# Moving three small tiles so that the 52 general slots start at another address residue

## The chip, the core and the metric

The kernel runs on one core of a Trainium2 chip. The metric is the device time of one execution in microseconds, as the median of several runs. TensorE does the matmuls, VectorE and ScalarE the elementwise work, GpSimd and SyncE mostly issue DMAs. All operands of TensorE come from SBUF, the on-chip memory, in which every tile has a start address that is the same in each of 128 partitions.

## What is computed

One inference step of a one-layer decoder: 2048 prompt positions with 16 learned tokens ahead of them, and 8 sample positions. Cut to what matters:

```python
h = rmsnorm(x); p = h @ w_in            # q | k | v | conv GLU a | conv GLU b
attn = sliding-window attention(q, k, v)  # 8 heads, window 128, sinks, relative bias
c = silu(layernorm(depthwise_conv(a * sigmoid(b), width=31)))
x = x + concat(attn, c) @ w_out         # 1024 -> 1024
x = x + relu(rmsnorm(x) @ w_up)**2 @ w_down   # 1024 -> 4096 -> 1024
y = rmsnorm_final(x)
```

All arrays are float32. The outputs are y for prompt and samples, and the new key, value and convolution states.

## The kernel before, in words

Activations lie with the channels on the partitions and the tokens along the row. The tokens are cut into five tiles of 384, 448, 448, 448 and 320 prompt positions; the first has 16 more columns in its input projection (400), the last 8 sample columns (328). The program goes through the tiles, and the feed-forward of one tile covers attention and convolution of the next, whose steps are dealt out between matmuls by generators.

Weights come as 86 slabs of 128 x 1024: 14 for the input projection, 8 for the output projection and 64 for the feed-forward (up and down). dma_slab loads a slab into raw, and split_slab splits it on ScalarE and VectorE into whi and wlo, two float32r tiles whose sum is the slab. Activations are split the same way into a high and a low tile. pe_step multiplies one slab with one tile: 24 matmuls, of which 16 have whi as weights against the high and the low activation of 8 chunks, and 8 have wlo against the high one. The moving operands are general slots in the input projection, up and down. In the output projection four of the eight chunks are parts of the tiles cah and cal (attention) and four are general slots (convolution).

SBUF is dealt out by pools in the order in which they are opened (lines 80 to 84): cp for constants, tp for the general slots, tm for temporaries, sl for weight slabs, at for attention and the rest. Inside a pool the tiles follow in the order of their first use. A general slot comes from slot() in line 140, is 128 x TS float32, and has the name t; TS is 448, and there are 52 of them. A temporary comes from tmp() in line 144, has the name m and 448 columns too; ss and rs are of the same size. The small parameters sm hold the norm gains, the taps and biases of the convolution and the sinks, 169 columns, and are read as scalars of one column by VectorE and ScalarE all through the program. The constants epst and sq0 have one column each, idn, ones and onesr 128 columns, bias 8 x 256. In tp, relt is the first user of a slot.

The order of the instructions on each engine comes from the framework's scheduler. x is loaded into slots by DMA from SyncE or GpSimd (load_x, line 339), and the result is stored from slots in final_gen (line 908), for the last tile from SyncE and ScalarE by turns.

Of the kernel before, what the change touches and what calls it, by code (L numbers as in the profile page):

```python
# [7 lines left out]
F32 = mybir.dt.float32  # L8
# [31 lines left out]
NSMALL = 169  # L40
# [36 lines left out]
def trunk(tc, x_in, w_all, smalls, rel, ck, cv, sconv, y_out, kv_out, ck_out, cv_out, up_out, us_out):  # L77
    nc = tc.nc
    with ExitStack() as ctx:
        cp = ctx.enter_context(tc.tile_pool(name="cp", bufs=1))  # L80
        tp = ctx.enter_context(tc.tile_pool(name="tp", bufs=NSLOT))
        tm = ctx.enter_context(tc.tile_pool(name="tm", bufs=NTMP))
# [46 lines left out]
        def act(out, a, f, bias=0.0, scale=1.0, accum_out=None):  # L129
            if accum_out is None:  # L130
                return nc.scalar.activation(out, a, f, bias=bias, scale=scale)  # L131
            return nc.scalar.activation(out, a, f, bias=bias, scale=scale, accum_out=accum_out)  # L132
# [22 lines left out]
        def mm(out, lhsT, rhs, start, stop):  # L155
            return nc.tensor.matmul(out, lhsT, rhs, start=start, stop=stop)  # L156

        sm = cp.tile([128, NSMALL], F32, name="sm")
        nc.scalar.dma_start(sm, smalls)
        relt = tp.tile([128, TM], F32, tag="t", name="relt")  # L160
        nc.gpsimd.dma_start(relt[:33, :8 + EW], rel)
# [1 line left out]
        make_identity(nc, idn)  # L163
        ones = cp.tile([128, 128], F32, name="ones")
        nc.vector.memset(ones, 1.0)
        epst = tm.tile([128, 1], F32, tag="epst", name="epst", bufs=1)
        nc.vector.memset(epst, EPS)
        sq0 = tm.tile([128, 1], F32, tag="sq0", name="sq0", bufs=1)
        act(sq0, epst, AF.Sqrt)
        bias = cp.tile([128, NH, 256], F32, name="bias")  # L170
        scr = dr.tile([NSMP, NH, EW], F32, name="scr")
# [1017 lines left out]
def build(shapes):  # L1189
    import concourse.bacc as bacc  # L1190

    nc = bacc.Bacc("TRN2", target_bir_lowering=False, num_devices=1, dynamic_dma_scratch_size=8192)
    args = [nc.dram_tensor(n, s, F32, kind="ExternalInput").ap() for n, s in shapes.items()]
    args += [nc.dram_tensor(n, s, F32, kind="ExternalOutput").ap() for n, s in _OUTS]
    with tile.TileContext(nc, schedule_with_timeline_sim=True) as tc:
        trunk(tc, *args)
    return nc
# [28 lines left out]
```

## Time and profile before

| | us |
|---|---|
| median of 3 runs | 2118.57 |
| lowest and highest of them | 2117.73, 2121.74 |
| profiled execution, whole | 2122.0 |
| profiled execution, span | 2120.2 |
| TensorE busy in the span | 2086.2 |
| VectorE busy | 1525.5 |
| ScalarE busy | 1180.9 |

The span runs from the first to the last instruction. Busy time of an engine is the time in which one of its instructions was running; matmuls overlap, and their ends are modelled, so the distance between their starts tells the pace and the duration doesn't. The chain is the work that ended last, followed back from the end.

### The profile page before, as it was taken

To read this page: it belongs to the slowest core of one execution; us is meant where nothing else is said; L and a number is where in the kernel's file an instruction comes from. 1 tells how busy PE (TensorE), PEld (TensorE's weight loads), DVE (VectorE), ACT (ScalarE), POOL (GpSimd) and SP (SyncE) were. 2 spreads that over 40 slices of the span, in tenths; PEclk is the share of its full clock that TensorE was granted. 3 is DMA by queue.
4 is the path that set the end of the run, shared out by engine and by line. 5 is a ranking of instruction groups with operands and counts; after the bars stand their busy time and mean duration, and the time that the engine had idled before them with its cause. 6 is when DMAs were issued, how large, how long until landed. Compare 5 with 4: busy or idle time off the path is not lost.

```text
span 2120.2 us, 29986 instructions
## 1 busy us (share of the span) xinstructions
PE 2086.2 (98%) x11338; PEld 1967.8 (93%) x11338; DVE 1525.5 (72%) x2595; ACT 1180.9 (56%) x2156; POOL 50.7 (2%) x98
## 2 busy tenths in 40 slices
PE   7899999999999999999999999999999999999998
PEld 7787999999999999999999999999999999999997
DVE  5897698987857987648669886566797754574444
ACT  6576465567456455565455647554646475454443
POOL 2000000000000000000000000000010100000000
PEclk9999999999999999999999999999999999999999
DMA  5112333334533222234432222244433322444443
GB/s 203 42 40 80 110 123 116 120 110 154 179 112 102 100 99 100 100 131 148 144 110 100 100 100 100 100 170 145 147 115 112 121 100 103 151 161 153 148 143 104
DMA packets 77328, 254.19 MB, mean 120 GB/s; under 512 B 9501, under 2 KB 19869, under 8 KB 77184
## 3 DMA queue, kind: packets, MB, share of 16 engines
q1 hardware_dynamic: 72000, 238.08, 32.6%
q0 software_dynamic: 4464, 13.45, 1.9%
q8 instruction: 89, 1.46, 0.3%
q10 hardware_dynamic: 720, 0.76, 0.1%
q14 instruction: 55, 0.45, 0.1%
HBM read 241.97 MB, written 10.28 MB: 119 GB/s over the span
## 4 chain that ended last, share of the span: by engine, by line
PE 97%; DVE 2%; DMA 1%; ACT 0%; issue 0%; SPq 0%; DVEq 0%; ACTq 0%
PE mm L156 91%; PE st L156 2%; PE s L156 1%; PE pt L581 1%; PE cps L156 1%; DVE t L116 1%; DMA raw<-w_all 0%; DVE t L112 0%; DMA sm<-smalls 0%; DVE m L116 0%; DVE wlo L112 0%; ACT bias L135 0%; DVE ss L112 0%; PE mx L156 0%; PE st L530 0%
## 5 line engine op out<-in xcount | busy, mean ns | idle before, releaser
L156 PE MATMUL mm<-t,whi 128*128 128x448 f32 (+3 forms) x6560 | 1347.6, 352 | 14.0 <-ACT t L131 8.9
L156 PEld LDWEIGHTS mm<-t,whi 128*128 128x128 f32 x6560 | 1173.9, 189 | 76.3 <-ACT t L131 9.9
L135 ACT CAST whi<-raw 128x1024 fp32r<-128x1024 f32 x424 | 443.7, 1049 | 561.9 <-PE mm L156 444.3
L156 PE MATMUL mm<-t,wlo 128*128 128x448 f32 (+3 forms) x3280 | 709.0, 349 | 0.0
L112 DVE TENSOR_TENSOR wlo<-raw,whi 128x1024 fp32r<-128x1024 f32 x424 | 517.1, 1220 | 244.3 <-PE mm L156 138.2
L156 PEld LDWEIGHTS mm<-t,wlo 128*128 128x128 f32 x3280 | 588.8, 188 | 29.8 <-issue 0.6
L116 DVE SCALAR_TENSOR_TENSOR t<-u,sm,t 128x448 f32<-128x448 f32 (+1 forms) x480 | 301.1, 646 | 3.5
L112 DVE TENSOR_TENSOR t<-mm,t 128x448 f32<-128x448 f32 (+2 forms) x200 | 116.8, 584 | 182.8 <-PE mm L156 179.8
L112 DVE TENSOR_TENSOR t<-m,t 128x448 fp32r<-128x448 f32 (+3 forms) x236 | 134.5, 583 | 26.3 <-ACT t L135 25.7
L135 ACT CAST t<-m 128x448 fp32r<-128x448 f32 (+3 forms) x236 | 125.4, 536 | 18.7 <-DVE m L116 14.6
L131 ACT ACTIVATE m<-mm 128x448 f32<-128x448 f32 (+2 forms) x176 | 90.1, 512 | 53.1 <-PE mm L156 51.2
L131 ACT ACTIVATE m<-t 128x448 f32<-128x448 f32 (+3 forms) x140 | 72.3, 543 | 60.8 <-DVE t L112 40.9
L131 ACT ACTIVATE m<-m 128x448 f32<-128x448 f32 (+3 forms) x164 | 90.1, 550 | 9.0 <-DVE m L112 5.1
L132 ACT ACTIVATE p<-p,nm 112x240 f32<-112x240 f32 (+3 forms) x152 | 72.3, 477 | 26.8 <-DVE nm L121 26.6
L562 DVE CUSTOM_DVE_ANT_0 p<-s,bias,sm 112x240 f32<-112x240 f32 (+3 forms) x152 | 61.3, 450 | 4.6 <-PE s L156 2.7
L131 ACT ACTIVATE p<-p,rd 112x240 f32<-112x240 f32 (+3 forms) x152 | 61.9, 476 | 3.7 <-DVE rd L127 3.0
L112 DVE TENSOR_TENSOR ss<-ss,m 128x448 f32<-128x448 f32 (+3 forms) x100 | 58.5, 585 | 6.9 <-ACT m L131 3.4
L127 DVE RECIPROCAL rs<-m 128x448 f32<-128x448 f32 (+2 forms) x15 | 41.6, 2776 | 24.0 <-ACT m L131 24.0
L116 DVE SCALAR_TENSOR_TENSOR t<-t,sm 128x384 f32<-128x384 f32 (+1 forms) x98 | 56.9, 613 | 2.4 <-ACT t L131 2.0
L156 PE MATMUL mm<-cah,whi 128*128 128x448 f32 (+2 forms) x160 | 55.6, 349 | 1.2 <-DVE t L116 1.2
L920 POOL DMA_DIRECT2D y_out<-t x32 | 17.3, 542 | 1632.6 <-DVE t L116 1631.2
L156 PE MATMUL mm<-cal,whi 128*128 128x448 f32 (+2 forms) x160 | 55.4, 348 | 0.0
(179 smaller groups left out, 1145.4 us busy)
## 6 DMA issues: line engine op xcount, KB each, us to landing
raw<-w_all SPq DMA_DIRECT2D x424, 512.0 KB, 3.2
t<-x_in SPq DMA_DIRECT2D x40, 224.0 KB, 4.3
y_out<-t POOLq DMA_DIRECT2D x24, 224.0 KB, 3.3
t<-x_in SPq DMA_DIRECT2D x16, 164.0 KB, 3.5
t<-x_in POOLq DMA_DIRECT2D x8, 224.0 KB, 6.5
t<-x_in SPq DMA_DIRECT2D x8, 200.0 KB, 5.2
t<-x_in SPq DMA_DIRECT2D x8, 192.0 KB, 4.4
y_out<-t POOLq DMA_DIRECT2D x8, 192.0 KB, 3.9
```

The costliest lines, as they stand in the source:

```text
L112: return nc.vector.tensor_tensor(out, a, b, op=op)
L116: return nc.vector.scalar_tensor_tensor(out, a, s, b, op0=op0, op1=op1)
L127: return nc.vector.reciprocal(out, a)
L131: return nc.scalar.activation(out, a, f, bias=bias, scale=scale)
L132: return nc.scalar.activation(out, a, f, bias=bias, scale=scale, accum_out=accum_out)
L135: return nc.scalar.copy(out, a)
L156: return nc.tensor.matmul(out, lhsT, rhs, start=start, stop=stop)
L562: nc.vector.tensor_tensor_reduce(out=p[:bq, c, :nk], in0=sp[c // 2][:bq, c % 2, :nk], in1=bias[:bq, h, b0:b0 + nk], scale=1.0, scalar=sm[: ...
L581: nc.tensor.transpose(t[:r, c * bq:(c + 1) * bq], p[:bq, c, a:a + r], idn[:bq, :bq])
L920: q.dma_start(y_out[:, YO[i] + c * n:YO[i] + (c + 1) * n], y[:, :n])
```

## The change

Three tiles change their pool. sm goes from cp to tm, where it is the first to be allocated, with a tag and one buffer of its own. epst and sq0 go from tm to cp, behind ones. Nothing that writes or reads them is changed. The general slots, in the pool between the two, get another start address.

```diff
-        sm = cp.tile([128, NSMALL], F32, name="sm")
+        sm = tm.tile([128, NSMALL], F32, tag="sm", name="sm", bufs=1)
         nc.scalar.dma_start(sm, smalls)
         relt = tp.tile([128, TM], F32, tag="t", name="relt")
...
         nc.vector.memset(ones, 1.0)
-        epst = tm.tile([128, 1], F32, tag="epst", name="epst", bufs=1)
+        epst = cp.tile([128, 1], F32, name="epst")
         nc.vector.memset(epst, EPS)
-        sq0 = tm.tile([128, 1], F32, tag="sq0", name="sq0", bufs=1)
+        sq0 = cp.tile([128, 1], F32, name="sq0")
         act(sq0, epst, AF.Sqrt)
```

## Rows read from the trace of the kernel before

**Rows 1.** The page: busy time by engine, and granted clock in 40 slices.
```profile
PE 2086.2 (98%) x11338; PEld 1967.8 (93%) x11338; DVE 1525.5 (72%) x2595; ACT 1180.9 (56%) x2156; POOL 50.7 (2%) x98
...
PEclk9999999999999999999999999999999999999999
```

**Rows 2.** The page: the chain's shares by engine, then by line.
```profile
PE 97%; DVE 2%; DMA 1%; ACT 0%; issue 0%; SPq 0%; DVEq 0%; ACTq 0%
PE mm L156 91%; PE st L156 2%; PE s L156 1%; PE pt L581 1%; PE cps L156 1%; DVE t L116 1%; DMA raw<-w_all 0%; DVE t L112 0%; DMA sm<-smalls 0%; DVE m L116 0%; DVE wlo L112 0%; ACT bias L135 0%; DVE ss L112 0%; PE mx L156 0%; PE st L530 0%
```

**Rows 3.** Chain in order of time: start us, length us, what, number of instructions.
```profile
275.20 12.75 PE mm L156 x72
...
322.57 13.87 PE mm L156 x80
...
410.85 17.82 PE mm L156 x102
...
662.81 14.56 PE mm L156 x72
...
1001.01 29.93 PE mm L156 x148
...
1892.86 214.81 PE mm L156 x1432
```

**Rows 4.** Groups by shape, matmuls of 448 columns: out<-moving,weights, busy us, mean ns.
```profile
L156 PE MATMUL mm<-t,whi 128*128 128x448 f32 x3936 | 867.5, 367 | 1.0 <-DVE m L112 1.0
...
L156 PE MATMUL mm<-t,wlo 128*128 128x448 f32 x1968 | 455.8, 365 | 0.0
...
L156 PE MATMUL mm<-cal,whi 128*128 128x448 f32 x96 | 34.9, 364 | 0.0
L156 PE MATMUL mm<-cah,whi 128*128 128x448 f32 x96 | 34.9, 364 | 0.0
...
L156 PE MATMUL mm<-cah,wlo 128*128 128x448 f32 x96 | 23.4, 366 | 0.0
```

**Rows 5.** Timeline of TensorE, an output step of 448 columns: start us, us.
```profile
1004.30 0.37 PE L156 MATMUL mm<-cah,whi 128*128 128x448 f32 x1
...
1005.91 1.78 PE L156 MATMUL mm<-t,whi 128*128 128x448 f32 x8
1007.52 0.98 PE L156 MATMUL mm<-cah,wlo 128*128 128x448 f32 x4
1008.34 0.98 PE L156 MATMUL mm<-t,wlo 128*128 128x448 f32 x4
1009.15 0.37 PE L156 MATMUL mm<-cah,whi 128*128 128x448 f32 x1
```

**Rows 6.** Timeline of TensorE, starts of two output steps of 328 columns.
```profile
1808.88 0.32 PE L156 MATMUL mm<-cah,whi 128*128 128x328 f32 x1
...
1812.46 0.32 PE L156 MATMUL mm<-cah,whi 128*128 128x328 f32 x1
```

**Rows 7.** Groups by shape, VectorE and ScalarE on slots (t) and temporaries.
```profile
L112 DVE TENSOR_TENSOR t<-m,t 128x448 fp32r<-128x448 f32 x144 | 87.4, 620 | 18.2 <-ACT t L135 17.8
L135 ACT CAST t<-m 128x448 fp32r<-128x448 f32 x144 | 80.7, 567 | 15.3 <-DVE m L116 12.8
...
L112 DVE TENSOR_TENSOR m<-ss,m 128x448 fp32r<-128x448 f32 x11 | 6.8, 622 | 1.6 <-ACT m L135 1.6
...
L135 ACT CAST m<-ss 128x448 fp32r<-128x448 f32 x11 | 6.2, 563 | 2.2 <-DVE ss L112 2.2
```

**Rows 8.** Chain in order of time, head of the program.
```profile
0.81 4.34 DMA sm<-smalls
...
6.25 9.77 DMA raw<-w_all
```

**Rows 9.** The page, DMA issues: size of each, median us to landing.
```profile
y_out<-t SPq DMA_DIRECT2D x4, 164.0 KB, 1.9
y_out<-t ACTq DMA_DIRECT2D x4, 164.0 KB, 1.9
...
sm<-smalls ACTq DMA_DIRECT2D x1, 84.5 KB, 4.3
...
relt<-rel POOLq DMA_DIRECT2D x1, 50.5 KB, 4.6
```

## The prediction, made before the changed kernel ran

> **What bounds the kernel now.** I read the page first: TensorE is busy 98% of a span of 2120.2 us, and its granted clock stands at nine tenths or more in all 40 slices [rows 1]. The chain of work that ended last agrees: 97% of it is TensorE, 91% the one matmul line of the helper mm [rows 2]. So the time is the number of matmuls times their pace, and a change of addresses matters if it changes that pace, or the short head and tail where TensorE waits. The chain in order of time gives the pace, as microseconds of an unbroken piece divided by its matmuls [rows 3]. With 448 columns it is 14.56 us / 72 = 202.2 ns, with 328 columns 214.81 / 1432 = 150.0 ns. With 384 columns it differs from piece to piece: 13.87 / 80 = 173.4 ns, 17.82 / 102 = 174.7 ns, 12.75 / 72 = 177.1 ns. The columns alone, one for each cycle at the level of 2.4 GHz, would be an estimated 186.7, 136.7 and 160.0 ns. The pace thus carries 15.5 ns a matmul on top of 448 columns, and 13.3 to 17.1 ns on top of the others. An address can only act on this excess.
>
> **The change part by part.** First where things lie, from the shapes in the code. Tiles are laid one after the other in the order in which their pools are opened, in steps of 32 bytes a partition. Ahead of the general slots there were sm (676, so 704 bytes), idn, ones and onesr (512 each) and bias (8192), 10432 bytes in all. Now there are idn, ones, onesr, bias and the two constants of 32 bytes, 9792 in all. The slots move down by 640 bytes, which is 128 modulo 256. As they land on 192, they were on 64. A slot is 448 x 4 = 1792 bytes, seven times 256, so all 52 lie alike before and after. Behind them, the pool tm loses 64 bytes and gains 704 in front of the tiles m, so m, ss, rs, the weights raw, whi and wlo, and all of the pool at stay where they were. Counting on from the slots: m, ss, rs and the weights lie at 128, and in the pool at, behind the two small rq tiles, cah and cal lie at 192. That is the useful fact. The output projection reads moving operands from cah and cal, at 192, and from slots, at 64, in the same step and against the same weights. The kernel before therefore already runs matmuls on the address class to which the slots go.
>
> The change adds no instruction, no wait and no byte. sm is still written once by the same DMA, in the same program position; epst and sq0 have the same writers and readers. Edits other than addresses cost nothing by count.
>
> 448 columns, three of the five tiles: 3 x 86 slabs x 24 = 6192 matmuls. Mean durations by shape are 367 and 365 ns for slots and 364, 364 and 366 ns for cah and cal [rows 4]. Durations overlap, so the pace is the test. One output step takes 8 matmuls from cah and cal from 1004.30 to 1005.91, 1.61 us; 8 from slots to 1007.52, 1.61 us; 4 from cah to 1008.34, 0.82 us; 4 from slots to 1009.15, 0.81 us [rows 5]. The whole step is 4.85 us, and a step with slots alone is 14.56 / 3 = 4.85 us [rows 3]. A longer piece of the chain, from 1001.01 on, has 148 matmuls, among them 48 on cah or cal in its four output steps, and runs at 29.93 / 148 = 202.2 ns [rows 3]. Half or a third of the operands at 192 changes nothing to a tenth of a nanosecond. I take 0 us for 6192 matmuls. The bounds are in the rivals, since no stretch has all operands at 192.
>
> 328 columns, the last tile: 86 x 24 = 2064 matmuls. An output step with half of its operands at 192 goes from 1808.88 to 1812.46, 3.58 us [rows 6]; a step on slots alone is 24 x 150.0 = 3.60 us [rows 3]. If the 0.02 us belong to the class 192 and double when all operands are there, the 78 steps that now use slots alone gain 0.04 and the 8 others 0.02 us: about 3.3 us at most by rows rounded to 0.01 us. If they belong to the switching between classes inside a step, the 8 output steps lose them, under 0.2 us. The bounds are -3.3 and +0.2 us. I take -0.6 us, near the second, since the 448 steps show no such gain.
>
> 384 columns, the first tile behind its input projection: 72 x 24 = 1728 matmuls. Three paces occur with all slots at one residue, so something else chooses among them, such as the instant at which an unbroken run starts. If the change makes every run take the fast one, it gains (174.3 - 173.4) x 1728 = 1.6 us against a mean near 174.3 ns, which I estimate from the pieces of the chain; if every run takes the slow one, it loses (177.1 - 174.3) x 1728 = 4.8 us. I take 0, as I see no reason for either.
>
> VectorE and ScalarE read and write slots too, but the same shapes take the same time on other classes. A CAST into a slot takes 567 ns and one from ss into m, both at 128, 563 ns; a subtraction into a slot takes 620 ns and one into m 622 ns [rows 7]. They are not the bound, and a few nanoseconds vanish under TensorE. The cover is missing at the head, where sm's DMA is 4.34 us of the chain, ahead of slabs whose DMA is 9.77 us [rows 8]. It writes the same 676 bytes a partition to another address. Its landing is 4.3 us and that of relt, the other small load of that moment, 4.6 us [rows 9]; I take 0, with that gap of 0.3 us as the bound either way. idn, ones, onesr and bias move too, all small operands; 0.
>
> The DMAs that fill slots run under matmuls. Of those that empty them, the last eight stand at the very end, with a landing of 1.9 us [rows 9], and nothing covers the last. By landings alone I take 0 for it, and as the rows of the two queues agree to their rounding, bounds of 0.1 us either way. [...]
>
> The sum: 0 (448) - 0.6 (328) + 0 (384) + 0 (other engines, head, tail) = -0.6 us. The profiled execution took 2122.0 us, 1.8 us around its span of 2120.2; it lies 3.4 us above the median of the runs, 2118.57, so the difference is put on the median: 2118.0 us.
>
> **The rivals.** Faster: the excess at 448 columns is due to the class of the slots. At 448 it is 15.5 ns, at 328 it is 13.3 ns. If the 2.2 ns between them are slips that a start at 64 causes and a start at 192 does not, the 5904 matmuls at 448 columns that read slots gain 13.0 us, giving 2105.6 us, or 2102.3 with the bound at 328. For it speaks that the excess is no multiple of the columns alone, and that the 328 output step is a little shorter [rows 6]. Against it speaks the unbroken 202.2 ns with a third of the operands at 192 [rows 3, 5].
>
> Slower: the slow pace of 384 columns, 177.1 against 173.4 ns, shows that a run can settle on a pace 2.1% worse [rows 3]. If slots at 192, now on the other side of weights at 128, settle there, the place is every step of the up and down projections. The price is 4.8 us on the first tile alone, giving 2123.4 us, and 202.2 x 0.021 = 4.3 ns x 5904 = 25 us on the 448 steps too, giving some 2148 us. It decides from about 1000 of the 5904 matmuls on, which are 4.3 us. For it speaks that steps on slots alone do fall into different paces; against it, that 448 columns never show a slow one in the pieces read, with either class.
>
> The change doesn't do what it says: if the allocator laid sm first or rounded otherwise, the slots would stay at 64 or go elsewhere, and the time would be 2118.6 us. It would then also move the pool at, which the arithmetic of shapes speaks against. The same number results if the program's order of instructions is untouched and the class is without effect, so only the addresses could tell the two apart.
>
> **How the numbers follow.** A measurement of this kernel can tell about 0.2%, 4.2 us, from no change. Forecast, within that: 0.55, together with 0.02 for a change that does nothing, its own range 2114.4 to 2122.8. Faster by the 448 excess, whole or in part: 0.24. Slower by a worse pace: 0.19, of which 0.08 for about the first tile alone, to 2124. The range goes from 2105, the whole faster rival without the bound at 328, to 2124, and leaves out some 0.03 below and 0.11 above, with some room for an error in the terms. Faster 0.24, same 0.57, slower 0.19.
>
> **What would show it.** Right: pieces of the chain with 448 columns still at 202.2 ns a matmul, 328 columns between 149 and 150, and the 384 pieces again a mix of the three paces. The faster rival is right if 448 columns come down towards 200 ns. The slower one is right if a 448 step takes more than 4.87 us in unbroken pieces. The prediction is wrong in its ground if the order of instructions on an engine differs, or if durations of VectorE or ScalarE on slots move by over 2%. An output step is the control: cah and cal haven't moved, and after the change all of its moving operands are at 192.

## The result and the profile after

The changed kernel takes 2107.14 us (median; 2106.55 to 2108.22) beside 2119.72 us for the kernel before on the same chip: a ratio of 0.9939, 95% interval 0.9923 to 0.9955, 12.6 us less. The span of the profiled execution went from 2120.2 to 2106.5 us. The time lies in the stated range, but not where the likeliest forecast put it: the faster rival happened, which the prediction had priced at 13.0 us, and the forecast of no measurable change was wrong.

The chain of work in order of time, after the change (start us, length us, what, number of matmuls), with pieces that answer to those of [rows 3]:

```profile
272.42 12.50 PE mm L156 x72
...
319.46 13.87 PE mm L156 x80
...
407.65 17.69 PE mm L156 x102
...
529.64 32.52 PE mm L156 x171
...
657.65 14.40 PE mm L156 x72
...
992.54 29.61 PE mm L156 x148
...
1459.75 31.42 PE mm L156 x208
...
1774.61 57.82 PE mm L156 x336
...
1877.65 216.40 PE mm L156 x1432
```

448 columns now run at 14.40 / 72 = 200.0 ns a matmul, in the piece with output steps too (29.61 / 148 = 200.1), where it was 202.2. 328 columns became slower: 216.40 / 1432 = 151.1 ns, from 150.0. The pieces with 384 columns lost their slow paces: 173.6, 173.4 and 173.4 ns.

Three of these pieces in the kernel before, to place the gain in time:

```profile
533.59 32.74 PE mm L156 x171
...
1472.84 31.20 PE mm L156 x208
...
1789.63 57.81 PE mm L156 x336
```

The gain is 3.95 us by the first of them (533.59 - 529.64), 13.09 by the second, 15.02 by the third and 15.21 at the start of the last one [rows 3]. Then the last tile gives some back, and 13.7 are left at the end. Worked out by shape it is 6192 x (202.2 - 200.0) = 13.6 us for 448 columns and 2064 x (151.1 - 150.0) = 2.3 us given back for 328. The rest, some 2.4 us, is the first tile. By the distances between starts over the whole kernel its 1728 matmuls of 384 columns went from 174.2 to 173.4 ns, 1.4 us, and its 336 of 400 columns from 183.0 to 180.1 ns, 1.0 us.

An output step of 448 columns after the change, on TensorE's timeline, beside [rows 5]:

```profile
995.79 0.36 PE L156 MATMUL mm<-cah,whi 128*128 128x448 f32 x1
...
997.38 1.76 PE L156 MATMUL mm<-t,whi 128*128 128x448 f32 x8
998.99 0.96 PE L156 MATMUL mm<-cah,wlo 128*128 128x448 f32 x4
999.78 0.96 PE L156 MATMUL mm<-t,wlo 128*128 128x448 f32 x4
1000.59 0.36 PE L156 MATMUL mm<-cah,whi 128*128 128x448 f32 x1
```

It takes 4.80 us instead of 4.85, and the part on cah and cal, which haven't moved, became shorter as well: 997.38 - 995.79 = 1.59 us instead of 1.61. So the pace of an operand also depends on its neighbours. The prediction read the old output step as if each operand showed its own pace. The single starts inside that old step, in the kernel before, show more than its sum:

```profile
1004.30 0.37 PE L156 MATMUL mm<-cah,whi 128*128 128x448 f32 x1
1004.50 0.37 PE L156 MATMUL mm<-cal,whi 128*128 128x448 f32 x1
1004.71 0.36 PE L156 MATMUL mm<-cah,whi 128*128 128x448 f32 x1
...
1005.91 1.78 PE L156 MATMUL mm<-t,whi 128*128 128x448 f32 x8
```

The first two matmuls on cah and cal take 0.41 us, 205 ns each, and the six after them 1.20 us, 200.0 ns each. The starts of 16 such steps agree: 203.5 ns for the first two, 200.0 for the next six, and 202.1 for the eight on slots behind them; the two blocks of four that follow run at 203.1 and 204.0. So operands at 192 were fast already, inside a block of eight, and what they won there was lost again around the changes between 192 and 64.

The other engines kept their durations (groups by shape, after, beside [rows 7]):

```profile
L112 DVE TENSOR_TENSOR t<-m,t 128x448 fp32r<-128x448 f32 x144 | 87.2, 618 | 18.2 <-ACT t L135 17.7
L135 ACT CAST t<-m 128x448 fp32r<-128x448 f32 x144 | 80.8, 567 | 16.4 <-DVE m L116 13.8
```

### The profile page after: what moved, and what is told of

Read it like the earlier page. It is cut to its first block, busy times and chain, and to the rows that moved or that the text cites. A ratio compares the mean times of both kernels' runs of the same rounds, so it can differ in the third digit from the quotient of the medians.

```text
span 2106.5 us, 29986 instructions
## 1 busy us (share of the span) xinstructions
PE 2071.0 (98%) x11338; PEld 1963.7 (93%) x11338; DVE 1524.4 (72%) x2595; ACT 1179.9 (56%) x2156; POOL 50.7 (2%) x98
## 4 chain that ended last, share of the span: by engine, by line
PE 97%; DVE 2%; DMA 1%; ACT 0%; issue 0%; SPq 0%; DVEq 0%; ACTq 0%
PE mm L156 90%; PE st L156 2%; PE s L156 1%; PE pt L581 1%; PE cps L156 1%; DVE t L116 1%; DMA raw<-w_all 0%; DVE m L116 0%; DVE t L112 0%; DVE wlo L112 0%; DMA sm<-smalls 0%; ACT bias L135 0%; DVE ss L112 0%; PE st L529 0%; PE st L530 0%
## 5 line engine op out<-in xcount | busy, mean ns | idle before, releaser
L112 DVE TENSOR_TENSOR t<-mm,t 128x448 f32<-128x448 f32 (+2 forms) x200 | 116.5, 582 | 176.3 <-PE mm L156 173.4
```

The costliest lines, as they stand in the source:

```text
L112: return nc.vector.tensor_tensor(out, a, b, op=op)
```

## The experiments

Theory A2, formed after the result: the pace is set by the distance from the weights to the moving operand (the start of the operand minus the start of the weights, in bytes modulo 256), and 64 is the good distance. Its rivals: A1, the residue of the moving operand itself counts; B, one of the tiles that were moved is the cause; C, accesses of other engines to the slots are. The first expectation's A stands for A1 and A2 together.

**Padding instead of moving.** Empty bytes behind the constants and ahead of the tiles m set the residue of the slots, and leave the residue of everything behind them:

```diff
-        ones = cp.tile([128, 128], F32, name="ones")
+        ones = cp.tile([128, 128], F32, name="ones"); cp.tile([128, 32], F32, name="padc"); tm.tile([128, 32], F32, tag="padt", name="padt", bufs=1)
```

This is pad192; pad0 has 48 and 16 columns, pad128 has 16 and 48.

> The kernel before, with 128 empty bytes behind the constants and 128 more ahead of the tiles m: sm, epst and sq0 stay where they were, the general slots lie at 192 modulo 256, and everything behind them keeps its residue. Theory A (the residue of the slots alone sets the pace of the matmuls): as the changed kernel, 2107 us within 3, 448 columns at 200.0 ns a matmul. Theory B (one of the tiles that the change moved, sm or a constant, is the cause): as the kernel before, 2119 us within 3, 448 columns at 202.2 ns.

> The kernel before with 192 empty bytes behind the constants and 64 ahead of m: slots at 0 modulo 256. Theory A1 (a start at 64 alone is bad): 2107 us within 4. Theory A2 (only the distance of 64 to the weights at 128, on the far side, is good): slots at 0 are 128 away from the weights, so the pace is another one, at least 202.2 ns at 448 columns, and the time 2119 us or more. Theory B: 2119 us.

> The kernel before with 64 empty bytes behind the constants and 192 ahead of m: slots at 128 modulo 256, the same residue as the weights. Theory A1 (a start at 64 alone is bad): 2107 us within 4. Theory A2 (slots that start at the residue of the weights collide most): above 2119 us, by as much as 2.1% of the 448 columns, some 25 us. Theory B: 2119 us.

| slots at | weights at | distance | kernel | us | ratio to before, interval |
|---|---|---|---|---|---|
| 64 | 128 | 192 | before | 2120.72 | |
| 192 | 128 | 64 | pad192 | 2107.30 | 0.9937 (0.9922 to 0.9952) |
| 0 | 128 | 128 | pad0 | 2133.23 | 1.0059 (1.0044 to 1.0074) |
| 128 | 128 | 0 | pad128 | 2129.39 | 1.0042 (1.0028 to 1.0056) |

pad192 has the whole gain with sm and both constants where they were, so B falls. Slots at 0 and at 128 are slower than slots at 64, so a start at 64 isn't the one bad residue. That slots at the residue of the weights collide most, as was expected of pad128, the times don't bear out: pad0 took longer. At 448 columns alone pad128 is the slower one, 204.4 against 203.8 ns by the starts over the whole kernel. The chain of pad0 and then of pad128:

```profile
664.70 14.69 PE mm L156 x72
```

```profile
899.41 14.59 PE mm L156 x72
914.77 9.92 PE mm L156 x48
...
1275.23 14.88 PE mm L156 x72
```

With slots at 0, 448 columns run at 14.69 / 72 = 204.0 ns. With slots at 128 there are two paces for the same addresses: 14.59 / 72 = 202.6 and 9.92 / 48 = 14.88 / 72 = 206.7 ns.

**Bare matmuls.** All of the kernel is left out but float32r matmuls from constant tiles, in one run. Its loops, in short:

```python
for n in (448, 400, 384, 328, 320):
    for w in "abcd":            # weights at 0, 64, 128, 192
        for m in "abcd":        # moving operand at 0, 64, 128, 192
            run(m, w, n, 48)    # 24 matmuls to a PSUM tile
```

> Leaves out the whole computation: only float32r matmuls from constant tiles, 48 for each of 5 numbers of columns (448, 400, 384, 328, 320), 4 residues of the weights and 4 of the moving operand (a, b, c, d for 0, 64, 128, 192 modulo 256). Then 8 starts in steps of 32 bytes against weights at 128, and moving operands at 64 and 192 by turns, and in the pattern of an output step. VectorE and ScalarE stand still. Theory A1 (residue of the moving operand alone): for 448 columns moving b is slow (202.2 ns) and d fast (200.0) whatever the weights. Theory A2 (distance between moving operand and weights): what is fast follows the difference, so against weights at 128 d is fast, against weights at 0 b is fast. Theory C (other engines' accesses to the slots make the difference): all 16 pairs run alike. Mixtures of 64 and 192: 202.2 ns as in the output steps of the kernel before, if one slow operand is enough; 201.1 ns if the pace is a mean over operands.

TensorE's timeline of micro1: a row starts where a pair starts, so the pace is the distance to the next row's start over 48. Letters a to d stand for 0, 64, 128 and 192:

```profile
77.17 9.89 PE L112 MATMUL mm<-mvb,wtb 128*128 128x448 f32 x48
86.89 9.77 PE L112 MATMUL mm<-mvc,wtb 128*128 128x448 f32 x48
96.50 9.95 PE L112 MATMUL mm<-mvd,wtb 128*128 128x448 f32 x48
106.28 9.95 PE L112 MATMUL mm<-mva,wtc 128*128 128x448 f32 x48
116.07 9.87 PE L112 MATMUL mm<-mvb,wtc 128*128 128x448 f32 x48
125.78 9.89 PE L112 MATMUL mm<-mvc,wtc 128*128 128x448 f32 x48
135.50 9.77 PE L112 MATMUL mm<-mvd,wtc 128*128 128x448 f32 x48
145.11 9.76 PE L112 MATMUL mm<-mva,wtd 128*128 128x448 f32 x48
154.71 9.95 PE L112 MATMUL mm<-mvb,wtd 128*128 128x448 f32 x48
```

Against weights at 128 (wtc) the moving residues 0, 64, 128 and 192 take 9.79, 9.71, 9.72 and 9.61 us, that is 204.0, 202.3, 202.5 and 200.2 ns. Against weights at 64 the fast one is 128 (mvc: 9.61 us), against weights at 192 it is 0 (mva: 9.60 us): the fast operand moves along with the weights, always 64 ahead. At a distance of 128 the pairs mvd, wtb and mva, wtc take 9.78 and 9.79 us. A1 falls, and so does C, since VectorE and ScalarE stood still.

Other numbers of columns follow the distance too, each in its own order. At 400 columns the distances 0 and 64 give 180.0 ns, 128 and 192 give 183.4, and at 384 columns 0 and 64 give 173.3, 192 gives 174.6 and 128 gives 176.1, all worked out from the starts inside the runs. The gain of the first tile fits these paces. At 328 columns 64 isn't good:

```profile
522.48 7.36 PE L112 MATMUL mm<-mvb,wtc 128*128 128x328 f32 x48
529.67 7.31 PE L112 MATMUL mm<-mvc,wtc 128*128 128x328 f32 x48
536.82 7.41 PE L112 MATMUL mm<-mvd,wtc 128*128 128x328 f32 x48
544.06 7.41 PE L112 MATMUL mm<-mva,wtd 128*128 128x328 f32 x48
```

A distance of 192 takes 7.19 us, 0 takes 7.15 and 64 takes 7.24. By the starts inside these runs that is 150.0, 148.9 and 151.1 ns; the last tile ran at 150.0 ns before the change, with 192, and at 151.1 after it, with 64. With 320 columns nothing of this is left:

```profile
629.32 7.20 PE L112 MATMUL mm<-mva,wtc 128*128 128x320 f32 x48
636.36 7.20 PE L112 MATMUL mm<-mvb,wtc 128*128 128x320 f32 x48
643.40 7.19 PE L112 MATMUL mm<-mvc,wtc 128*128 128x320 f32 x48
650.43 7.20 PE L112 MATMUL mm<-mvd,wtc 128*128 128x320 f32 x48
```

These start 7.03 or 7.04 us apart, some 146.6 ns a matmul at any distance. In the mixtures behind them, against weights at 128, operands at 64 and 192 by turns ran at 203.4 ns, and the pattern of an output step at 202.2 ns, both worked out from the starts of single matmuls: as slow as or slower than operands at 64 alone.

**The weights moved instead of the slots.** The strongest test of A2 in the whole kernel:

```diff
-        ones = cp.tile([128, 128], F32, name="ones")
+        ones = cp.tile([128, 128], F32, name="ones"); sl.tile([128, 32], F32, tag="padw", name="padw", bufs=1)
```

> The kernel before with 128 empty bytes ahead of the weight tiles: the slots and all constants stay where they were, slots at 64 modulo 256, but raw, whi and wlo go from 128 to 0, and cah and cal from 192 to 64. The moving operands are again 64 bytes past the weights modulo 256, without having moved. Theory A2 (distance from weights to moving operand): as the changed kernel, 2107 us within 3, 448 columns at 200.0 ns, 328 at 151.1 ns. Theory A1 (residue of the moving operand): as the kernel before, 2119 us within 3.

2107.88 us, ratio 0.9943 (0.9928 to 0.9958). The chain:

```profile
656.61 14.40 PE mm L156 x72
...
1876.81 216.39 PE mm L156 x1432
```

These are the paces of the changed kernel, 200.0 and 151.1 ns, with the slots still at 64. So are sm and all constants where they were, also onesr and bias, which had moved along with the slots in the changed kernel and in pad192. The distance is the cause, for 448 and for 328 columns.

**The mixed step.** The changed kernel with the pool named at, which holds cah and cal, moved by 128 bytes. That puts cah and cal back on the slow distance, 192 from the weights, and leaves the slots:

```diff
-        ones = cp.tile([128, 128], F32, name="ones")
+        ones = cp.tile([128, 128], F32, name="ones"); at.tile([128, 32], F32, tag="pada", name="pada", bufs=1)
```

> The changed kernel with 128 empty bytes ahead of cah: slots and weights stay (192 and 128), cah and cal go to 64, so that half of the operands of an output step are on the slow class. If one slow class in a step sets its pace: output steps of 448 columns at 202.2 ns a matmul, as in the kernel before, and up and down steps still at 200.0. If the pace is a mean over the operands: output steps at 201.1 ns. In both cases at most 1.3 us more than the changed kernel.

Its timeline of TensorE, two starts of an output step and the parts between:

```profile
995.85 0.36 PE L156 MATMUL mm<-cah,whi 128*128 128x448 f32 x1
...
997.06 1.77 PE L156 MATMUL mm<-t,whi 128*128 128x448 f32 x8
998.67 0.98 PE L156 MATMUL mm<-cah,wlo 128*128 128x448 f32 x4
999.49 0.97 PE L156 MATMUL mm<-t,wlo 128*128 128x448 f32 x4
...
1001.92 1.77 PE L156 MATMUL mm<-t,whi 128*128 128x448 f32 x8
```

From one t,whi row to the next is a step: 1001.92 - 997.06 = 4.86 us, 202.5 ns a matmul, with half of the operands on the fast distance. In 16 such steps of the run it was 4.85 to 4.86 us. So one slow class among the operands takes the gain from the whole step. A mean over operands would have been 4.83 us. The execution took 2108.45 us, one run.

**A version for the last tile.** The distance 64 costs the last tile 1.1 ns a matmul. A slot has 448 columns and this tile uses 328, so its moving operands can start further right:

```diff
+        def mslot(n):
+            return slot(F32R)[:, MSH.get(n, 0):]
...
-                hi.append(slot(F32R))
-                lo.append(slot(F32R))
+                hi.append(mslot(n))
+                lo.append(mslot(n))
...
-            st[i]["cah"], st[i]["cal"] = ch, cl
+            k = MSH.get(RT[i], 0)
+            st[i]["cah"], st[i]["cal"] = ch[:, :, k:], cl[:, :, k:]
...
+MSH = {328: 40}
```

The hidden layer (hh, hl) and the convolution's chunks use mslot in the same way. 40 columns give a start at 96, 48 (best128) one at 128.

> The changed kernel, with the moving operands of the last tile (328 columns) 40 columns further to the right in their slots and in cah and cal, so that they start at 96 modulo 256 instead of 192; slots, weights and the other tiles stay. From the bare matmuls, 146.7 ns at 96 against 151.1 ns at 192 in the changed kernel: 2064 x 4.4 ns = 9.1 us less, 2098 us within 3. Rival (other engines' accesses, which the bare matmuls lack, spoil it): 2107 us.

> As best328, but the moving operands of the last tile start 48 columns further to the right, at 128 modulo 256, the residue of the weights. Both series of bare matmuls and the kernel with all slots at 128 gave 148.8 to 149.0 ns there, without a second pace: 2064 x (151.1 - 148.9) ns = 4.5 us less than the changed kernel, 2103 us within 2. Rival (the pace hangs on how a run starts, as at 96): 2107 us or more.

The last long piece of the chain, best328 and then best128:

```profile
1874.26 219.59 PE mm L159 x1432
```

```profile
1876.23 214.81 PE mm L159 x1432
```

best328 missed: 2109.49 us, a ratio to the kernel before of 0.9948 (0.9935 to 0.9960), as its up and down steps ran at 219.59 / 1432 = 153.3 ns, not 146.7. Its output steps did reach 146.7, worked out from their starts. best128 ran at 150.0 ns, between the 148.9 expected and the 151.1 of its rival, and took 2104.99 us, 0.9931 (0.9917 to 0.9946): 2.2 us below the changed kernel, as 2064 x 1.1 ns gives. Measured against the kernel before in each case, their intervals overlap, so that best128 is the faster of the two rests on the piece, 214.81 against 216.40 us, rather than on the times.

**Finer starts, and how a run starts.** Two more series of bare matmuls with weights at 128, one run each. micro2 has starts in steps of 16 bytes; micro3 has one matmul of 16 to 256 columns ahead of each run, which shifts its first instant (448 columns from 192: 0.03 us behind the start of one of 16 columns, 0.11 us behind one of 256):

```python
for n, k in ((448, 48), (448, 32), (448, 16), (328, 24), (328, 32)):  # start at 4 k bytes
    for q in range(1, 17):
        mark(16 * q)        # one matmul of 16 q columns
        ...                 # 48 matmuls of n columns
```

> Leaves out the whole computation: only float32r matmuls with weights at 128 modulo 256 and one moving tile that starts at 0, 16, 32 and so on to 240, for 448, 400, 384 and 328 columns, 48 matmuls each. If lines of 64 bytes decide, starts inside a line run alike, save for the columns left over at the ends; if finer steps decide, some start is faster than 200.0 ns for 448, 180.0 for 400 or 173.3 for 384 columns.

> Leaves out the whole computation: only float32r matmuls with weights at 128 modulo 256. Five cases (448 columns from 192, 128 and 64; 328 columns from 96 and 128), each 16 times with 48 matmuls behind one other matmul of 16, 32 and so on to 256 columns, which shifts the instant at which the run starts. If the pace hangs on the two addresses alone: one pace a case. If it also hangs on how a run starts: more than one in the cases in which two have been seen (448 from 128: 202.8 and 206.7 ns; 328 from 96: 146.7, 150.2 and 153.3; 328 from 128: 148.9 and 150.0), and one, 200.0 ns, for 448 from 192, which showed no other in any kernel.

In micro2 no start beat 200.0, 180.0 and 173.2 ns for 448, 400 and 384 columns. In this series only 144 and 192 reach 200.0 with 448 columns, and 16, 32, 160 and 240 run at 206.7; but in micro1 32 and 160 did run at 200.0. These starts have more than one pace, so whether starts inside the same 64 bytes are alike is not settled.

In micro3 (timeline of TensorE), 448 columns from 128 and 328 columns from 96, neighbouring runs:

```profile
263.47 9.94 PE L130 MATMUL mm<-mvs,wtc 128*128 128x448 f32 x48
...
273.32 10.11 PE L130 MATMUL mm<-mvs,wtc 128*128 128x448 f32 x48
...
585.88 7.25 PE L130 MATMUL mm<-mvs,wtc 128*128 128x328 f32 x48
...
593.07 7.53 PE L130 MATMUL mm<-mvs,wtc 128*128 128x328 f32 x48
```

The addresses are the same and only the length of the one matmul ahead differs, and yet 48 matmuls take 0.17 and 0.28 us more. By the starts inside the runs, 448 columns from 128 run at 202.5 to 202.8 ns in 11 of 16 runs and at 206.7 in 5; 328 columns from 96 at 146.7 in 14 and at 153.3 in 2; 328 from 128 between 148.7 and 151.0. 448 columns from 192 run at 199.9 to 200.1 ns in all 16, and from 64 at 202.0 to 202.4. So the gain of the change rests on a pace that didn't hang on how a run starts in any of these runs, and the 146.7 ns that best328 was built on does hang on it.

## Why the prediction was right or wrong

**What bounds the kernel**: right. The same 11338 matmuls at another pace are the whole difference, and the order of the instructions is the same on every engine.

**Where things lie**: right, as pad192 gives the same time as the change by setting the residue alone. The sum shown leaves one thing out: 10432 bytes alone would put the slots at 192 modulo 256, and 9792 at 64. They lie at 64 and 192, since the first pool itself begins at 128 modulo 256 in the kernel as built. In every distance this drops out.

**448 columns, taken as 0 us**: the failed step. It read "half or a third of the operands at 192 changes nothing" from mixed output steps, and carried it over to steps with all operands at 192. cah64 shows that a mixed step runs at the slow pace, 202.5 ns, whichever half is slow. The sums over blocks in [rows 5] could not tell the two theories apart; the single starts inside them could, 200.0 ns at 192 from the third matmul of a block of eight on. With all operands at 192 every step of 448 columns came down from 202.2 to 200.0 ns. That no stretch had all operands at 192 was noticed, and put into the rivals instead of the term. It was worth 13.6 us.

**328 columns, -0.6 us with bounds of -3.3 and +0.2**: wrong in sign and outside its bounds. It measured +2.3 us, for the same reason: the 3.58 us of the mixed step belong to the mixture, and wt0 gives 151.1 ns at the same distance again.

**384 columns, 0 with bounds of -1.6 and +4.8 us**: inside the bounds near the lower end, at -1.4 us; the pieces at 174.7 and 177.1 ns went to 173.4 and 173.6. It was taken as 0 for want of a reason; micro1 shows one, 173.3 ns at the distance 64 against 174.6 at 192. What chose among the paces before was said to be perhaps the instant at which a run starts; micro3 shows that an instant can, for other shapes, and for this one it isn't shown. The 400 columns of the first input projection had no term of their own, and gained 1.0 us.

**Other engines, 0**: right. A CAST into a slot took 567 ns before and after, a subtraction 620 and 618.

**Head and tail, 0**: right within their bounds. sm's DMA took 4.17 us of the chain instead of 4.34, the first slab 10.08 instead of 9.77, and TensorE's first piece of the chain starts at 17.13 instead of 17.14 us. The last stores landed in 1.9 us, as in [rows 9].

**The faster rival, 2105.6 us at 0.24**: it happened, and the time fell into the range because this rival had set its lower end. The time is 1.5 us above its price, of which 1.15 us are the kernel before, at 2119.72 us here and not at 2118.57; the change itself gave 12.6 us against 13.0. Two terms that the price lacked nearly cancel, 2.3 us lost at 328 columns and some 2.4 us won on the first tile. The price came from the 2.2 ns that 448 columns carry over 328 on top of the columns alone, taken as 186.7 and 136.7 ns; micro1 shows the 0.417 ns a column that these come to, (200.0 - 146.6) / 128 from 320 to 448 columns. And 2.2 ns is what 448 columns lost. That the two agree is in part luck: the 13.3 ns at 328 columns are no floor, as the same change made 151.1 - 136.7 = 14.4 ns of them. Its reason was half right: a class of slots caused the 2.2 ns, though not the start at 64 but the distance of 192 to the weights.

**The slower rival**: its mechanism exists, a run that settles on a worse pace, by 2.0% in pad128 (206.7 against 202.6 ns) and by 4.5% in best328 (153.3 against 146.7). At the distance of 64 with 448 columns it occurred in none of these runs.

## What to carry to other kernels

In a kernel bound by back-to-back float32r matmuls, where the moving operand starts relative to its weights, modulo 256 bytes, is a parameter to try: here it was worth between -0.6% and +0.6% without any more instructions. The good distance belongs to a number of columns: of the four in micro1, 64 is the best for 448 columns (200.2 ns, the others 202.3 to 204.0) and slower than 0 and 192 for 328 (151.1 ns against 148.9 and 150.0). Read its effect only from steps in which every operand has the same distance, since one slow class hid the gain of the others (202.5 ns in cah64, 200.0 in the changed kernel); an experiment of bare matmuls shows all pairs in one run. Prefer a pair whose pace stays the same when the instant of its start is shifted (448 columns from 192: 199.9 to 200.1 ns in micro3) over one that is faster in a single run (328 columns from 96: 146.7 or 153.3 ns).

## What the runs showed of the hardware that was not expected

In micro1, at a granted clock of 1.00, the best paces of four numbers of columns, by the starts inside the runs, lie on a straight line: 200.0 ns for 448, 180.0 for 400, 173.3 for 384 and 146.6 for 320. That is (200.0 - 146.6) / 128 = 0.417 ns a column and 13.2 ns on top of the columns for each of the four. 328 columns also ran at 146.7 ns in micro3, 9.9 ns on top, so the 13.2 ns are not a floor. That the distance between moving operand and weights counts needs no other engine at work: micro1 has it too, 204.0 against 200.2 ns with the moving operand at 0 and at 192 and the weights at 128. What inside TensorE or SBUF makes the distance count, and what in a start picks one of two paces, these runs don't show; that stays open.
